# Cross-attention of a streaming encoder layer on one core: weights folded into keys and values per head, token rows run through it once, sample rows moved into the feed-forward layer

## The chip, the cores and the metric

The kernel runs on one core of a Trainium2 chip. The metric is device time in microseconds (us); lower is better. A time is the median of several executions. A profile is of one further execution, and its "span" runs from the first to the last instruction.

The engines: TensorE (PE in the profile, with its weight loads as PEld), VectorE (DVE), ScalarE (ACT), GpSimd (POOL) and SyncE (SP), which here only issues DMAs.

## What is computed

One layer of an encoder, for 2048 prompt rows and 32 sample rows of width 1024: a mixer (band attention with 8 heads beside gated linear attention with 4 heads, and an output projection w_o), cross-attention to 256 memory tokens, and a SwiGLU feed-forward layer of width 2816. Each part is normed before and after and added to the rows. The change is in the cross-attention:

```python
def mem_kv(mem, g_mem, w_mk, w_mv):          # prompt; the sample rows have cached k, v
    m = rmsnorm(mem, g_mem)
    k = (m @ w_mk).reshape(n, 256, 4, 256)   # 4 heads of 256
    v = (m @ w_mv).reshape(n, 256, 4, 256)

def mem_attention(h, k, v, w_mq, w_mo):
    q = (h @ w_mq).reshape(n, t, 4, 256)
    s = einsum('nqhd,nkhd->nhqk', q, k) * 256 ** -0.5
    p = softmax(s)
    o = einsum('nhqk,nkhd->nqhd', p, v).reshape(n, t, 1024)
    return o @ w_mo

xp = xp + rmsnorm(mem_attention(rmsnorm(xp, g_pre_mem), mk, mv, w_mq, w_mo), g_post_mem)
xp = xp + rmsnorm(swiglu(rmsnorm(xp, g_pre_ffn), ...), g_post_ffn)
```

The keys and values of the memory are outputs too. Everything is f32.

## The kernel before

**Arithmetic.** Nearly every product is three matmuls (`mm3`): each f32 operand is split into a rounded part hi (type fp32r) and a rest lo, and hi\*hi + hi\*lo + lo\*hi is summed in PSUM. A split (L424, L425; L429, L430 in place) is a cast on ACT and a subtraction on DVE or POOL. Some small products run on plain f32 operands; the trace shows each of those as two records.

**Order.** Nothing runs in the order of the text. `Order` (top of the file) reads all traced instructions, gives each a cost and a latency, and schedules them onto the engines in passes, by the length of what follows. It respects how many buffers a tag has, the order in which the tiles of one tag are allocated, and memory: a pool that lies where a closed pool lay waits until that pool's work is done. The resulting order is then fixed for each engine, SP's DMA queue included. `high_priority` sets only the first pass's priorities.

**Stages**, with their times in the trace:

1. Input projections (`fm_unit`, `tm_unit`), to about 580 us.
2. The band stage, to about 1275 us: four row blocks (`BLK`, 512, 512, 512, 544 rows), each with band attention (`band_group`: tiles s, pt, po), linear attention (`gla_tile`: g_...), and dense work that a hand-written loop sprinkles between the units in "steps". In block 0 that is the memory's keys and values (`mem_kv`, tiles mkps and mvps); in blocks 1 to 3 it is the output projection of the block before (`out_proj`, wops), which ends in two norms and stores the rows (`x1d`) and the normed rows (`h1d`).
3. Behind the loop: `mem_q0`, the memory queries of the first 416 rows, and `out_proj` of block 3, to 1352 us.
4. The memory stage, 1352 to 1821 us, over five blocks of 416 rows (`CB`; 32 of the last are the sample rows). `mem_q` projects the next block's queries with w_mq (mqps) and stores them to DRAM; `mem_attn` runs, per head, scores of tiles of 104 rows (ms), softmax (mst, mpr), transposes (mpt) and values (mpv); `mem_out` multiplies by w_mo (mops), and `mem_fin` norms twice and stores rows (`x2d`) and normed rows (`h2d`). The weights w_mq and w_mo are loaded and split anew in every block (`load_w`, `w_piece`): 16 pieces of 128x512 per matrix and block. Heads and next queries are woven together in the text.
5. The feed-forward layer, from 1822 us, in three blocks (`CF`) of two column halves (348 or 346), with a seven-product scheme for 2x2 blocks (`seven_mov`, `seven_sta`; tiles pg, pu, pd). Its weights pass through four raw buffers (tag `wraw`, pool cwr) and eight split ones (`wsp`). Seven operands mf, each with a pool of its own, are made from `h2d` before a block starts.

## Time and profile before

| | us |
|---|---|
| median of 3 runs | 3236.2 |
| lowest and highest | 3235.85, 3237.94 |
| the profiled execution | 3241.13 |
| its span | 3239.3 |
| PE busy in the span | 3110.5 |
| the five stages end at about | 580, 1275, 1352, 1821, 3239 |

The profile's views used here: the page (shares of the engines, the chain of work that ended last, groups of instructions), the groups by line in a window, windows (busy time of each engine in a stretch), and the timeline of one engine. A group's row has the line, engine, operation, `out<-in` by the program's names, shape and count; then busy time and the mean length of one in ns; then the engine's idle time just before and who ended it. A timeline row has start and length in us, and in brackets the idle time before it. Matmuls overlap: a matmul's own length is more than its distance from the next one.

### The profile page before, as it was taken

The numbers are of one execution on the slowest core, as the hardware profiler recorded it, in microseconds if no ns is written. First come the engines' busy times: TensorE is split into PE (matmuls) and PEld (weight loads), VectorE is DVE, ScalarE is ACT, GpSimd is POOL, SyncE is SP. The second block draws the span as 40 slices with busy tenths as digits, with TensorE's granted clock in tenths as the row PEclk, the third lists the DMA queues.
The fourth block names the chain that finished last, engine by engine and source line by source line (L and its number), as shares of the span: only waits on it lengthen the run. The fifth ranks groups of instructions, "written<-read, shape, count | busy, mean of one in ns | idle before, by whom it ended". The sixth has DMA issues, their size and how long they took to land.

```text
span 3239.3 us, 57597 instructions
## 1 busy us (share of the span) xinstructions
PE 3110.5 (96%) x21027; PEld 2969.1 (92%) x21027; DVE 2448.5 (76%) x4513; ACT 1709.8 (53%) x3656; POOL 751.6 (23%) x912
## 2 busy tenths in 40 slices
PE   7898999799999999999999799999999999999998
PEld 7888999698888888999999799999889999999997
DVE  7875976476575756678776988888987778987776
ACT  5654655556576756566655554444443334543333
POOL 0200100245374546411010111111041111121111
PEclk9999999999999999999999899999999999999999
DMA  5559374785585756766653644544454445444444
GB/s 149 179 159 298 103 208 130 253 250 181 173 273 165 222 175 200 226 203 207 202 180 118 198 159 167 172 166 166 146 201 143 143 143 170 116 167 144 143 143 161
DMA packets 515261, 575.44 MB, mean 178 GB/s; under 512 B 81952, under 2 KB 431305, under 8 KB 514977
## 3 DMA queue, kind: packets, MB, share of 16 engines
q1 hardware_dynamic: 514977, 571.76, 55.9%
q8 instruction: 166, 2.72, 0.4%
q14 instruction: 118, 0.97, 0.1%
HBM read 422.21 MB, written 150.53 MB: 177 GB/s over the span
## 4 chain that ended last, share of the span: by engine, by line
PE 86%; DVE 5%; DMA 3%; issue 2%; ACT 2%; SPq 1%; POOL 1%; DVEq 0%; POOLq 0%; ACTq 0%
PE pg_X L485 7%; PE pu_X L485 7%; PE pdX L485 7%; PE wops L1330 6%; PE mops L485 6%; PE mqps L485 4%; PE po L1064 4%; PE pg_Y L485 4%; PE pu_Y L485 4%; PE pdY L485 3%; PE s L1059 2%; PE pt L1084 2%; PE pg_Z L485 2%; PE pu_Z L485 2%; PE g_s L1264 2%
## 5 line engine op out<-in xcount | busy, mean ns | idle before, releaser
L425 POOL TENSOR_TENSOR u<-g,u 128x692 fp32r<-128x692 f32 (+1 forms) x111 | 199.0, 1799 | 1043.3 <-ACT u L424 862.6
L485 PE MATMUL pg_X<-mf,wg_s 128*128 128x346 f32 (+1 forms) x1584 | 281.6, 325 | 12.8 <-DVE mf L425 6.3
L485 PE MATMUL pu_X<-mf,wu_s 128*128 128x346 f32 (+1 forms) x1584 | 278.9, 323 | 1.4 <-DVE up L533 1.0
L485 PEld LDWEIGHTS pg_X<-mf,wg_s 128*128 128x128 f32 x1584 | 258.8, 191 | 17.0 <-DVE mf L425 6.6
L485 PEld LDWEIGHTS pu_X<-mf,wu_s 128*128 128x128 f32 x1584 | 257.9, 190 | 2.6 <-DVE up L533 1.3
L485 PE MATMUL pdX<-u,wd 128*128 128x346 f32 (+1 forms) x1440 | 241.2, 326 | 10.3 <-issue 7.3
L485 PEld LDWEIGHTS pdX<-u,wd 128*128 128x128 f32 x1440 | 234.8, 192 | 12.6 <-issue 8.3
L424 ACT CAST wg_s<-wg_r 128x512 fp32r<-128x512 f32 x231 | 136.7, 620 | 191.1 <-DVE wg_r L530 91.7
L1330 PE MATMUL wops<-om,wo_s 128*128 128x512 f32 (+1 forms) x960 | 214.4, 362 | 0.4 <-POOL om L430 0.4
L424 ACT CAST u<-g 128x692 fp32r<-128x692 f32 (+1 forms) x111 | 84.2, 773 | 231.2 <-PE pdX L485 171.7
L485 PE MATMUL mops<-mo,wmo_s 128*128 128x416 f32 x960 | 192.1, 353 | 2.1 <-DVE y L1672 2.1
L425 DVE TENSOR_TENSOR wu_s<-wu_r,wu_s 128x512 fp32r<-128x512 f32 x231 | 166.9, 746 | 27.3 <-ACT wu_s L424 27.1
L424 ACT CAST wu_s<-wu_r 128x512 fp32r<-128x512 f32 x231 | 136.9, 621 | 86.1 <-DVE wu_r L530 38.2
L485 PEld LDWEIGHTS mops<-mo,wmo_s 128*128 128x128 f32 x960 | 177.3, 188 | 5.0 <-issue 3.4
L425 DVE TENSOR_TENSOR wg_s<-wg_r,wg_s 128x512 fp32r<-128x512 f32 x231 | 155.1, 693 | 31.5 <-ACT wg_s L424 31.1
L485 PE MATMUL mqps<-m,wmq_s 128*128 128x416 f32 x768 | 164.4, 359 | 5.3 <-DVE m L430 5.3
L1330 PEld LDWEIGHTS wops<-om,wo_s 128*128 128x128 f32 x960 | 149.3, 188 | 20.4 <-issue 2.2
L1064 PE MATMUL po<-prt,v 128*128 128x128 f32 x1120 | 158.7, 282 | 2.2 <-DMA v<-vad 1.3
L1064 PEld LDWEIGHTS po<-prt,v 128*128 128x128 f32 x1120 | 146.0, 195 | 10.1 <-issue 2.2
L485 PEld LDWEIGHTS mqps<-m,wmq_s 128*128 128x128 f32 x768 | 141.0, 191 | 6.9 <-DVE m L430 5.5
L485 PE MATMUL pg_Y<-mf,wg_s 128*128 128x346 f32 (+1 forms) x792 | 141.1, 326 | 1.7 <-ACT wg_s L424 1.4
L533 DVE TENSOR_TENSOR acc<-acc,pdX 128x346 f32<-128x346 f32 (+1 forms) x192 | 96.4, 513 | 59.1 <-PE pdX L485 58.6
(468 smaller groups left out, 7807.1 us busy)
## 6 DMA issues: line engine op xcount, KB each, us to landing
wd<-wdd SPq DMA_DIRECT2D x140, 512.0 KB, 4.8
wdd<-wd SPq DMA_DIRECT2D x70, 512.0 KB, 3.2
wg_r<-in_w_ffn_gate_dram SPq DMA_DIRECT2D x66, 512.0 KB, 4.4
wu_r<-in_w_ffn_up_dram SPq DMA_DIRECT2D x66, 512.0 KB, 4.7
wmq_r<-in_w_mq_dram SPq DMA_DIRECT2D x80, 256.0 KB, 3.3
wmo_r<-in_w_mo_dram SPq DMA_DIRECT2D x80, 256.0 KB, 3.3
q<-qd SPq DMA_DIRECT2D x32, 512.0 KB, 4.9
wo_r<-in_w_o_dram SPq DMA_DIRECT2D x64, 256.0 KB, 4.0
```

Source lines behind the costliest of these rows:

```text
L424: ACT.copy(hi, src)
L425: (lo_eng or DVE).tensor_tensor(out=lo, in0=src, in1=hi.bitcast(F32), op=ALU.subtract)
L485: PE.matmul(ps, lhsT=a, rhs=b, start=first and i == 0, stop=last and i == len(seq) - 1, skip_group_check=skip)
L533: eng.tensor_tensor(out=out, in0=a, in1=b, op=ALU.add)
L1059: PE.matmul(ps_out, lhsT=q[:, 2 * i + e, q0 : q0 + nq], rhs=ks[:, e, k0 : k0 + ncol], start=i == 0, stop=i == 1)
L1064: PE.matmul(po[:, e * P : e * P + n], lhsT=v[:kk, j, e * 64 : e * 64 + P], rhs=prt[:kk, j, :n], start=j == 0, stop=j == len(rows) - 1)
L1084: PE.transpose(ptp[:kk, j, :n], pr[:n, c0 : c0 + kk], ident[:n, :n])
L1264: PE.matmul(sps[bk, li, :], lhsT=lh, rhs=rh, start=True, stop=True)
L1330: PE.matmul(ps, lhsT=a, rhs=b, start=i == 0, stop=i == len(seq) - 1)
```

## The change

For head h let Wq_h be the 256 columns of w_mq that make its queries, and Wo_h the 256 rows of w_mo that take its output. The scores are h Wq_h k_h^T, so `keys_fold` forms Wq_h k_h^T (1024x256) once for each head; the four together are `gT`, 1024x1024. The output is p_h v_h Wo_h, so `values_fold` forms v_h Wo_h (256x1024) once for each head; the four together are `hT`. Both are split and stay in SBUF (64 KB of each partition apiece). The host passes w_mq a second time, transposed, and the values come out transposed.

- In the band loop only the keys remain in block 0's dense work. The split operand of the memory goes to DRAM (`mmd`) and is read again; the value projection runs behind the loop. `mem_q0` goes. The folding of the keys is woven into the last `out_proj`, the folding of the values follows, then that block's norms.
- The memory stage runs over the 2048 prompt rows alone: `token_tile` takes 128 rows through scores (two halves of 512 columns, two heads each), softmax and transposes; `output` takes 256 rows through the product with hT, the two norms and the stores. `output` comes one quarter late, and its two norm parts are placed between later token tiles.
- The 32 sample rows are handled by `sample()`, a generator advanced once after each `gate_up` of the feed-forward's first block. It multiplies with plain f32 operands and the rows as the stationary side (32 columns), K chunks going in turn to the four partition quarters of one PSUM bank; the quarters are summed by a product with a stacked identity (`fold`). Its weights pass through the feed-forward's raw buffers.
- Pools may now lie at either end of the memory (`side="right"`), so that what follows lies over what is free first. The last two operands' pools (cm5, cm6) lie over the outputs y, four others (cm1 to cm4) mostly over hT. The DRAM blocks `CB` become those of the feed-forward, whose first operands are made in one go of 1392 columns instead of two of 696.
- `Order` learns of the two ends, of several new tiles of one tag in an instruction, and prices a plain f32 matmul of 512 columns and 32 result rows as one of four that run side by side.

The core of the diff:

```diff
+                if n == 512 and list(outs[0].ap)[0][1] == 32:
+                    return n * 0.42, 300.0
...
-    CB = [(i * 416, 416) for i in range(5)]
+    CF = [(0, 348), (696, 346), (1388, 346)]
+    CB = [(s, 2 * n) for s, n in CF]
...
+            return [first] + [partial(key, m) for m in range(KT)], [again] + [partial(value, m) for m in range(KT)]
+        def keys_fold(h):
+            kt = fold_head(mkd, h, "kt")
+            for a in range(2):
+                w = fold_w(ins["w_mq_t"], h, a, "wqt")
+                for i2 in range(2):
+                    ps = psc.tile([P, 512], F32, tag="sc", name=f"gps{h}{a}{i2}")
+                    for i in range(2):
+                        c0 = (2 * i2 + i) * P
+                        mm3(ps[:, i * NMEM : i * NMEM + NMEM], [((w[j][0][:, 0, c0 : c0 + P], w[j][1][:, 0, c0 : c0 + P]), (kt[:, 0, j * NMEM : j * NMEM + NMEM], kt[:, 1, j * NMEM : j * NMEM + NMEM])) for j in range(2)])
...
+        def values_fold(h):
+            vt = fold_head(mvd, h, "vt")
+            for a in range(2):
+                w = fold_w(ins["w_mo"][0], h, a, "wov")
+                for t in range(2):
+                    ps = psc.tile([P, 512], F32, tag="sc", name=f"hps{h}{a}{t}")
+                    mm3(ps, [((vt[:, 0, j * NMEM + t * P : j * NMEM + t * P + P], vt[:, 1, j * NMEM + t * P : j * NMEM + t * P + P]), (w[j][0][:, 0], w[j][1][:, 0])) for j in range(2)])
...
-        for _ in steps(q0 + outp[3][0] + outp[3][1]):
+        for _ in steps(vals):
+            pass
+        att.close()
...
+        for _ in steps(outp[3][0] + weave(outp[3][1], [partial(keys_fold, h) for h in range(HM)])):
+            pass
+        amm.close()
+        kh_ = pool("bhm", 1, **RT)
+        hT = kh_.tile([P, 2, KT, D], F32R, name="hT")
+        for _ in steps([partial(values_fold, h) for h in range(HM)]):
...
+        def token_tile(i, c, pT):
+            ht = load_h(i, c)
+            cs = slice(c * P, c * P + P)
+            row = kvp.tile([P, 2, 512], F32, tag="kv", name=f"mpr{i}_{c}")
+            for hf in range(2):
+                ps = psc.tile([P, 512], F32, tag="sc", name=f"ms{i}_{c}_{hf}")
+                gs = slice(hf * 512, hf * 512 + 512)
+                mm3(ps, [((ht[:, 0, k], ht[:, 1, k]), (gT[:, 0, k, gs], gT[:, 1, k, gs])) for k in range(KT)])
+                st = sp.tile([P, 8], F32, tag="st8", name=f"mst{i}_{c}_{hf}", bufs=4)
+                pr = row[:, hf]
+                softmax(pr, ps, P, st, 2)
+                tr = ptr.tile([P, 4, P], F32, tag="tr", name=f"mpt{i}_{c}_{hf}")
+                for j in range(4):
+                    PE.transpose(tr[:, j], pr[:, j * P : j * P + P], ident)
+                if c == 0:
+                    pT.append(tp.tile([P, 2, HK, 256], F32R, tag="pT", name=f"pT{i}_{hf}"))
+                split(pT[hf][:, 0, :, cs], pT[hf][:, 1, :, cs], tr, DVE)
...
+            for m4 in range(2):
+                pss = [py.tile([P, 512], F32, tag="out", name=f"mo{i}_{2 * m4 + j}") for j in range(2)]
+                for e in range(2):
+                    for hf in range(2):
                         for j in range(2):
+                            c = slice((4 * m4 + 2 * j + e) * P, (4 * m4 + 2 * j + e) * P + P)
+                            mm3(pss[j][:, e * 256 : e * 256 + 256], [((hT[:, 0, hf * HK + k, c], hT[:, 1, hf * HK + k, c]), (pT[hf][:, 0, k], pT[hf][:, 1, k])) for k in range(HK)], hf == 0, hf == 1)
...
+        for i in range(NQ):
+            pT = []
+            token_tile(i, 0, pT)
+            for f in fins:
+                next(f, None)
+            token_tile(i, 1, pT)
+            for f in fins:
+                next(f, None)
+            if pend is not None:
+                fins = [output(i - 1, pend)]
+                next(fins[-1], None)
+            pend = pT
...
+        mps = {i: pool(f"cm{i}", 1, **RT) for i in range(5)}
...
+        mps.update({i: pool(f"cm{i}", 1) for i in (5, 6)})
...
+            def proj(src, mov, name):
+                part = uu.tile([P, 2, 512], F32, tag="u", name=name + "_p")
+                for hf in range(2):
+                    ps = pd.tile([P, 512], F32, tag="dense", name=f"{name}_a{hf}")
+                    for k2 in range(KT // 2):
+                        w = wr.tile([P, 2, 512], F32, tag="wraw", name=f"{name}w{hf}{k2}", bufs=WRB)
+                        SP.dma_start(w, src[2 * k2 * P : (2 * k2 + 2) * P, hf * 512 : hf * 512 + 512].rearrange("(k p) m -> p k m", p=P))
+                        for e in range(2):
+                            j = (2 * k2 + e) % 4
+                            PE.matmul(ps[j * TS : j * TS + TS], lhsT=mov[:, 2 * k2 + e], rhs=w[:, e], start=k2 < 2, stop=k2 >= 2)
+                    (DVE.tensor_copy if hf else ACT.copy)(part[:, hf], ps)
+                ps = pd.tile([P, 512], F32, tag="dense", name=name)[:, : KT * TS].rearrange("p (m t) -> p m t", m=KT)
+                for m in range(KT):
+                    PE.matmul(ps[:, m], lhsT=part[:, m // HK, m % HK * P : m % HK * P + P], rhs=fold, start=True, stop=True)
+                return ps
...
             for g in range(NG):
                 held.append(gate_up(g))
+                next(own, None)
```

More of the change, by code (lines that the diff above doesn't have):

```diff
@@ L296, in _pass @@
                         _, i = heappop(heap)
-                        stop = None
-                        for k in self.uses[i]:
+                        stop, new = None, {}
+                        for k in sorted((k for k in self.uses[i] if not held[k]), key=place.get):
                             g = self.tag[k]
-                            if not held[k] and (free[g] <= 0 or head[g] != place[k] or (back is None and self.first[k] != i)):
+                            c = new.get(g, 0)
+                            new[g] = c + 1
+                            if free[g] <= c or head[g] + c != place[k] or (back is None and self.first[k] != i):
                                 stop = g
@@ new lines, in value @@
+            def value(m):
+                w = load_w(wp, ins["w_mv"][0], m * P, P, f"wmv{m}")
+                ps = pd.tile([P, 512], F32, tag="dense", name=f"mvps{m}")
+                yield from mm3_steps(ps[:, :NMEM], [(w[k], (mv[k][:, 0, :NMEM], mv[k][:, 1, :NMEM])) for k in range(KT)], 12)
+                vf = sp.tile([P, 544], F32, tag="st", name=f"mvf{m}")
+                DVE.tensor_copy(vf[:, :NMEM], ps[:, :NMEM])
+                SP.dma_start(mvd[m * P : (m + 1) * P, :], vf[:, :NMEM])
+                SP.dma_start(outs["mv_t"][m * P : (m + 1) * P, :], vf[:, :NMEM])
@@ new lines, in softmax @@
+        def softmax(pr, ps, n, st, heads):
+            DVE.tensor_reduce(out=st[:n, 0:heads], in_=ps.rearrange("p (h j) -> p h j", h=heads), axis=AX.X, op=ALU.max, negate=True)
+            for h in range(heads):
+                c = slice(h * NMEM, h * NMEM + NMEM)
+                ACT.activation(pr[:n, c], ps[:, c], AF.Exp, bias=st[:n, h : h + 1], accum_out=st[:n, 2 + h : 3 + h])
+            DVE.reciprocal(st[:n, 4 : 4 + heads], st[:n, 2 : 2 + heads])
+            for h in range(heads):
+                c = slice(h * NMEM, h * NMEM + NMEM)
+                DVE.tensor_scalar(out=pr[:n, c], in0=pr[:n, c], scalar1=st[:n, 4 + h : 5 + h], scalar2=None, op0=ALU.mult)
@@ new lines, in encoder_step @@
+        NQ = TP // 256
+        pend, fins = None, []
+        for i in range(NQ):
[10 more added lines that the diff above has]
+            pend = pT
+        fins.append(output(NQ - 1, pend))
+        for f in fins:
+            for _ in f:
+                pass
@@ L1809, in encoder_step @@
+        own = sample()
         late = []
```

453 lines of the change are left out of this document (218 added, 235 removed).

## The prediction

> **What bounds the kernel now.** First the shares of the engines and the chain that ended last (the page's parts 1 and 4):
>
> ```profile
> PE 3110.5 (96%) x21027; PEld 2969.1 (92%) x21027; DVE 2448.5 (76%) x4513; ACT 1709.8 (53%) x3656; POOL 751.6 (23%) x912
> PE 86%; DVE 5%; DMA 3%; issue 2%; ACT 2%; SPq 1%; POOL 1%; DVEq 0%; POOLq 0%; ACTq 0%
> ```
>
> TensorE is busy for 96% of the span and makes up 86% of the chain. But "busy" here includes matmuls that overlap their own tails, so I check it stage by stage. The windows below cover the first band block, the passage to the last w_o projection, the memory stage, the passage to the feed-forward layer, and its first block:
>
> ```profile
> 590.00:758.00 168.00, 156.42 (x1542) 138.19 (x1543) 118.03 (x322) 106.76 (x306) 76.67 (x168) 0.97 0.76 239
> 1255.00:1352.00 97.00, 96.79 (x674) 94.37 (x673) 53.29 (x88) 54.63 (x120) 38.29 (x33) 1.00 0.75 236
> 1352.00:1821.00 469.00, 461.37 (x2660) 444.73 (x2658) 360.27 (x682) 281.09 (x643) 74.23 (x57) 0.99 0.62 188
> 1821.00:1846.00 25.00, 9.49 (x26) 7.22 (x27) 24.46 (x33) 14.08 (x23) 3.82 (x2) 0.55 0.46 127
> 1846.00:2300.00 454.00, 446.75 (x2747) 440.86 (x2746) 400.11 (x657) 211.75 (x389) 73.94 (x41) 0.99 0.49 168
> ```
>
> The columns are the length, then the busy time and count of PE, PEld, DVE, ACT and POOL, then the granted clock, the DMA share and GB/s. The change replaces the 469 us of the memory stage. These are its matmul groups, from the groups by line in that window:
>
> ```profile
> L485 PE MATMUL mops<-mo,wmo_s 128*128 128x416 f32 x960 | 192.1, 353 | 2.1 <-DVE y L1672 2.1
> L485 PE MATMUL mqps<-m,wmq_s 128*128 128x416 f32 x768 | 164.4, 359 | 5.3 <-DVE m L430 5.3
> L485 PE MATMUL ms<-kTp,q 128*104 128x256 f32 (+1 forms) x456 | 73.6, 289 | 0.1
> L485 PE MATMUL mpv<-prR,vTp 128*128 128x416 f32 (+1 forms) x240 | 56.1, 352 | 0.0
> ```
>
> What one matmul costs is its distance from the next, not its own 350 ns. I read that from unbroken runs in the timeline of PE (start, length, operation, count):
>
> ```profile
> 1274.68 29.77 PE L1330 MATMUL mqps<-hq,wmq_s 128*128 128x416 f32 x156
> 1304.28 48.10 PE L1330 MATMUL wops<-om,wo_s 128*128 128x272 f32 x384
> 1352.22 0.92 PE L485 MATMUL mqps<-m,wmq_s 128*128 128x416 f32 x4
> ...
> 1364.58 1.57 PE L485 MATMUL ms<-kTp,q 128*104 128x256 f32 x12
> 1365.99 2.80 PE L485 MATMUL mqps<-m,wmq_s 128*128 128x416 f32 x14
> ...
> 1721.28 1.05 PE L1636 MATMUL ms<-ksT,qf 128*32 128x256 f32 x4
> 1722.26 0.44 PE L1645 MATMUL mpt<-ident,mpr 128*128 128x128 f32 x2
> ...
> 1734.00 0.53 PE L1655 MATMUL mpv<-prT,vs 128*128 128x32 f32 x4
> ```
>
> - 416 columns: (1304.28 - 1274.68) / 156 = **0.1897 us**. 272 columns: (1352.22 - 1304.28) / 384 = 0.1248. So a column costs 0.00045 us, and 512 columns extrapolate to **0.233**, 384 to 0.175.
> - 256 columns: (1365.99 - 1364.58) / 12 = **0.1175**.
> - Matmuls on plain f32 operands show as two records each. Two of 256 columns took 1722.26 - 1721.28 = 0.98, so **0.49** each. Two of 32 columns took 0.53 with their tail; I take 0.2 each.
>
> The old stage adds up: 768 x 0.1897 = 145.7 (queries of blocks 1 to 4), 960 x 0.1897 = 182.1 (w_mo), 456 x 0.1175 = 53.6 (scores), 192 x 0.1897 + 48 x 0.175 = 44.8 (values), 7.1 for the sample rows (8 x 0.49 + 16 x 0.2), and some 25 for transposes and all-ones matmuls. That is 458 of 469 us, so the stage is filled with matmuls almost throughout, and removing matmul time there removes span.
>
> **The change, part by part.** PE work that goes: queries 960 x 0.1897 = 182.1 (block 0's 192 run before 1352), w_mo 182.1, scores 53.6, values 44.8, sample rows 7.1: **469.7 us**.
>
> PE work that comes:
> - prompt scores against the folded keys, 16 tiles x 2 halves x 8 x 3 = 768 of 512 columns: 179.0;
> - outputs against the folded values, 8 quarters x 8 x 8 x 3 = 1536 of 256 columns: 180.5;
> - the folds, 192 of 256 columns (22.6) and 96 of 512 (22.4).
>
> Together **404.5 us**, 65 less. The 160 transposes and ten all-ones matmuls become 128 and sixteen shorter ones; I take these as equal. The value projection (192 of 256 columns, 22.6) keeps its size and moves behind the band.
>
> The sample rows come back in the feed-forward layer: 64 plain f32 matmuls of 32 result rows and 512 columns, 32 of 32 columns (6.4), 8 of 256 (3.9), transposes and norms 1.5. The 64 are the large unknown. One after another they cost 2 x 0.49 = 0.98 each, **63 us**. They write to the four partition quarters in turn; side by side in fours they cost **16**. The trace has small matmuls on separate parts of the array, and narrow ones on 32 rows of result:
>
> ```profile
> 551.86 1.56 PE L485 MATMUL wvb_T<-wvb_s,tail 128*32 128x256 f32 x12
> 553.25 1.57 PE L485 MATMUL wvb_T<-wvb_sx,tail 128*32 128x256 f32 x12
> 554.66 4.42 PE L485 MATMUL wvb_Y<-wvb_s,mi 128*128 128x256 f32 x36
> ...
> 1233.39 0.85 PE L1264 MATMUL g_s<-g_W 64*64 64x64 f32 x22
> ```
>
> The g_s records on 64x64 quarters start (0.85 - 0.22) / 21 = 0.03 us apart, the 0.22 being one record's own length. Serially, a plain f32 record of 64 columns would take 0.98 / 4 / 4 = 0.061. So they do run beside each other, at least two at a time, which puts the 64 near 31 us. Records as short as 0.03 us may be held by issue rather than by the array, so I go below that row, to **20**. The Trainium skill, "TensorE: Matmul & The Clock Gate", Part 3, gives three column tiles of 32 at N=512 a speedup of 2.38. An estimate by it, with four tiles at the same efficiency (3.2), would also be 20; no run here shows that form.
>
> Sample rows in all 31.8, so PE has 65 - 32 = **33 us** less.
>
> DVE and ACT lose the repeated splits of w_mq and w_mo, which each block made anew:
>
> ```profile
> L425 DVE TENSOR_TENSOR wmo_s<-wmo_r,wmo_s 128x512 fp32r<-128x512 f32 x80 | 55.8, 703 | 22.1 <-ACT wmo_s L424 20.6
> L425 DVE TENSOR_TENSOR wmq_s<-wmq_r,wmq_s 128x512 fp32r<-128x512 f32 x62 | 48.0, 780 | 14.6 <-ACT wmq_s L424 13.7
> ```
>
> Of DVE's 360 us in the stage these are 104; the folds need 32 such splits, some 23 us. Softmax and norm work per token stays, so DVE has about 280 us beside 405 of PE, and PE stays the bound. In the feed-forward's first block DVE is at 400 of 454 us; the sample rows bring some 40 short instructions, about 10 us (estimate: 0.25 each, from the 0.35 and 0.42 of 256 columns quoted under the rivals), in a stage that they lengthen by more. That costs nothing; with that cover gone it costs those 10. SP loses 160 weight loads of 256 KB for 32 such and 16 of 512 KB, and gains eight of 512 KB by which the projection's operand goes out and comes back; its queue holds 1% of the chain. The 16 pass through the four raw buffers of the gate and up weights, so a late sample matmul holds a gate load behind it; the planner sees this, and I put nothing on it.
>
> **Stalls that go, and that come.** These waits stand in the stage now:
>
> ```profile
> 1374.24 7.77 PE L485 MATMUL mqps<-m,wmq_s 128*128 128x416 f32 x26 [5.27 <-DVE m L430]
> ...
> 1797.23 14.40 PE L485 MATMUL mops<-mo,wmo_s 128*128 128x416 f32 x75 [2.07 <-DVE y L1672]
> ...
> 1833.62 1.82 PE L485 MATMUL pg_X<-mf,wg_s 128*128 128x348 f32 x5 [6.25 <-DVE mf L425]
> ...
> 1842.26 1.76 PE L448 MATMUL n_ps<-n_acc,ones 128*128 128x416 f32 x2 [5.66 <-POOL n_acc L446]
> ```
>
> After the 5.27 us wait, 26 matmuls took 7.77 us where 4.9 is their price, so that wait costs 8.2 us in all. The wait at 1797 costs 2.1. In the window from 1821 to 1846 PE issued 26 records, worth about 5 us at the next window's 454 / 2747 = 0.165: **20 us** lost. Sum 30.
>
> What comes:
> - First band block: the value projection was 22.6 us of filling in a window where PE is the busiest engine with 156 of 168 us. If PE holds that block, moving it costs 0; if the linear-attention chain does, up to 22.6. PE being ahead of DVE's 118, I take **6**.
> - Before the last w_o projection PE had 29.6 us of queries to do (the row at 1274.68) while its operands came:
>
> ```profile
> 1292.11 10.78 POOL L430 TENSOR_TENSOR om<-om 128x544 fp32r<-128x544 f32 x7 [0.26 <-ACT om L429]
> ```
>
>   The first of them is ready at 1292, so from 1274.7 some 18 us need filling. There are 22.6 us of values (part used earlier) and one key fold (5.7); the later folds queue behind w_o's weights. 0 to 18, I take **3**.
> - Start of the token tiles: a tile's operand (load, ACT, POOL) comes just as the tile before it ends; 0 to 8, I take **3**.
> - Passage to the feed-forward: its operands lie where the folded values lay, and the last two where the outputs lie that the last quarter's two norms still need. Their eight casts and subtractions of 1392 columns start only with the last output matmul. I keep the 20 of now; the sample query projection, whose buffers are free earlier, can run in that gap, and I let it fill 8. **12** (0 to 30).
>
> Sum 24 against 30. The span changes by -33 - 6 = -39. The profiled execution took 3241.1 us and lies 4.9 above the median of 3236.2 us, so 3241.1 - 39 - 4.9 = **3197 us**.
>
> **Rivals.** (a) The column tiles run one after another: 63 instead of 20, so 3240. For it: the 128x32 rows at 551.86 cost as much per matmul as 128x128 ones; against it: those all lie on one quarter, and g_s overlaps. (b) Each change of tile shape empties the array. One record outlasts its pitch by about 0.16 us (350 ns against 190); if the planner alternates the 64 with full matmuls, 128 changes cost 20, so 3217. Against it: 12 narrow ones at 551.86 and 12 at 553.25 take 1.39 and 1.41, just 12 x 0.1175, so no drain shows at these borders. The Trainium skill, "TensorEngine Tiling (Array Packing)", Key Properties, states that drain as a rule; here the trace doesn't agree. (c) The gain goes back into holes: the band block keeps its time (+17) and the 18 us stay empty (+15): 3229. (d) **Slower**: the softmax chain paces the token loop. Per half tile it is a reduction, two exponentials, a reciprocal and two scalings:
>
> ```profile
> L1638 DVE TENSOR_REDUCE mst<-ms 128x1 f32<-128x256 f32 x12 | 5.0, 422 | 5.2 <-PE ms L485 5.1
> L1640 ACT ACTIVATE mpr<-ms,mst 128x256 f32<-128x256 f32 x12 | 5.7, 475 | 1.1 <-DVE mst L1638 0.8
> L1642 DVE TENSOR_SCALAR mpr<-mpr,mst 128x256 f32<-128x256 f32 x12 | 4.2, 353 | 0.4
> ```
>
> With two of each, transposes and the split of 512 columns this is about 4.7 us, and there are 32 halves. Above 39 / 32 = 1.2 us exposed per half the gain is gone; at half the chain, 2.4 us, it costs 75: 3272. Against it: the same chain is hidden now (0.1 us of idle before 456 score matmuls, 0.0 before mpv), and three score banks and a whole quarter of output work lie beside it. (e) More than forecast: no holes, and the passage filled: 3197 - 24 = 3173.
>
> **How the numbers follow.** Forecast 3197 with its own range 3180 to 3215: 0.50. (a) 0.10, (b) 0.06, (c) 0.14, (d) 0.09, (e) 0.11. A difference of 0.2% (6.5 us) is about what a measurement of this kernel can tell. Faster: forecast, (b), (e) and most of (c), 0.77. Same: (a) and the rest of (c), 0.14. Slower: (d), 0.09. The range of 3168 to 3238 leaves out (d), half of (a) and a little below (e), 0.18.
>
> **What would show it.** Between the band and the first pg_X the new profile should hold 768 score matmuls near 0.233 apart and 1536 output matmuls near 0.1175, with few idle entries; the 64 narrow matmuls should start about 0.25 to 0.3 us apart; the window of the passage should hold a gap near 12 us; wops of block 0 should start 15 us or more before 758. The forecast is wrong if the narrow matmuls stand near 1 us apart, if idle time on DVE or ACT stands before the transposes of the token tiles, or if that first w_o projection starts no earlier than now.

## The result, and the profile after

| | before | after |
|---|---|---|
| median of 4 runs, us | 3236.45 | 3201.76 |
| lowest and highest | 3235.85, 3237.94 | 3201.33, 3202.80 |
| span of the profiled execution | 3239.3 | 3199.6 |

The ratio is 0.9893, with a 95% interval of 0.9875 to 0.991: 34.7 us less, where 39 were forecast (3197). The profiled execution of the kernel before lay 4.7 us above its median, so the spans differ by more, 39.7. The sum came out near; the account below shows that several of its terms did not.

From the page of the kernel after (engines: busy time, share of the span, instructions; then the chain's shares by engine; then two groups):

```profile
PE 3076.3 (96%) x21091; PEld 2884.7 (90%) x21091; DVE 2303.6 (72%) x4226; ACT 1584.9 (50%) x3338; POOL 770.5 (24%) x912
...
PE 88%; DVE 6%; ACT 2%; DMA 2%; issue 1%; SPq 1%; POOL 0%; DVEq 0%; ACTq 0%; POOLq 0%
...
L471 PE MATMUL ms<-gT,hm 128*128 128x512 f32 x768 | 190.5, 401 | 1.7 <-POOL hm L436 1.5
L471 PE MATMUL mo<-pT,hT 128*128 128x256 f32 x1536 | 191.4, 283 | 0.1
```

PE is still the engine that the chain runs on. The two last rows are the new memory stage: 768 score and 1536 output matmuls, as counted, with 1.8 us of idle time before all of them. PE's longest waits in the token tiles name a norm's sum (acc, 3.0 us in all) and a tile's operand (hm, 1.5); the softmax is named once, with 0.2 us, so rival (d) did not come. Four stretches of the same kernel, as windows (columns as in the prediction: length, PE, PEld, DVE, ACT, POOL, clock, DMA share, GB/s):

```profile
1357.80:1747.10 389.30, 384.60 (x2464) 345.60 (x2465) 194.08 (x373) 133.02 (x297) 89.86 (x55) 1.00 0.35 106
...
1747.10:1776.60 29.50, 23.91 (x128) 21.41 (x126) 28.51 (x42) 18.68 (x30) 7.28 (x4) 0.94 0.34 112
1747.10:2259.20 512.10, 493.03 (x2947) 463.81 (x2946) 426.33 (x696) 233.01 (x423) 72.40 (x41) 0.98 0.50 167
2259.20:2728.30 469.10, 453.02 (x2790) 449.21 (x2790) 374.11 (x603) 197.38 (x356) 83.53 (x53) 0.98 0.47 153
```

They are the token tiles, the passage to the feed-forward layer, its block 0 (the passage is its beginning), and its block 1. Cut at marks that both kernels have (the first wops, ms and pg_X matmul, read from the timelines), the 39.7 us between the two spans fall like this. "Forecast" puts the prediction's own terms into these stretches:

| stretch of the span | before, us | after, us | change | forecast |
|---|---|---|---|---|
| start to the first w_o matmul | 758.0 | 722.2 | -35.8 | -16.6 (values -22.6, band +6) |
| to the first score matmul | 595.0 | 635.6 | +40.6 | +34.2 (values +22.6, folds +45, block 0's queries -36.4, hole +3) |
| token tiles | 469.6 | 389.3 | -80.3 | -81 (matmuls -433.3 and +359.5, stalls -10.3 and +3) |
| feed-forward block 0 | 480.1 | 512.1 | +32.0 | +24 (sample rows +31.8, passage -8) |
| the rest | 936.6 | 940.4 | +3.8 | 0 |

The token tiles are right to within 1 us. The first two stretches are off by 19 and 6 in opposite directions, block 0 by 8. Of the -35.8, 2.7 us lie in the input projections, which end at 583.0 and 580.3: their matmuls are the same, and in the fourteen profiles here that mark lies anywhere from 578.8 to 584.3. The experiments take up the rest.

### The profile page after: what moved, and what is told of

Its sections match the earlier page's. It is cut to its first block, busy times and chain, and to the rows that moved or that the text cites. A ratio compares the mean times of both kernels' runs of the same rounds, so it can differ in the third digit from the quotient of the medians.

```text
span 3199.6 us, 56225 instructions
## 1 busy us (share of the span) xinstructions
PE 3076.3 (96%) x21091; PEld 2884.7 (90%) x21091; DVE 2303.6 (72%) x4226; ACT 1584.9 (50%) x3338; POOL 770.5 (24%) x912
## 4 chain that ended last, share of the span: by engine, by line
PE 88%; DVE 6%; ACT 2%; DMA 2%; issue 1%; SPq 1%; POOL 0%; DVEq 0%; ACTq 0%; POOLq 0%
PE pu_X L471 8%; PE pg_X L471 7%; PE pdX L471 7%; PE wops L1327 6%; PE ms L471 5%; PE mo L471 5%; PE po L1061 4%; PE pu_Y L471 4%; PE pg_Y L471 4%; PE pdY L471 4%; PE s L1056 2%; PE pt L1081 2%; PE pu_Z L471 2%; PE pg_Z L471 2%; PE g_s L1261 2%; PE pdZ L471 2%
## 5 line engine op out<-in xcount | busy, mean ns | idle before, releaser
L471 PE MATMUL ms<-gT,hm 128*128 128x512 f32 x768 | 190.5, 401 | 1.7 <-POOL hm L436 1.5
L471 PE MATMUL mo<-pT,hT 128*128 128x256 f32 x1536 | 191.4, 283 | 0.1
L471 PEld LDWEIGHTS mo<-pT,hT 128*128 128x128 f32 x1536 | 185.7, 188 | 1.6 <-DVE my L1661 0.3
L471 PEld LDWEIGHTS ms<-gT,hm 128*128 128x128 f32 x768 | 142.5, 189 | 34.8 <-POOL hm L436 1.9
L471 PE MATMUL pu_Y<-mf,wu_s 128*128 128x346 f32 (+1 forms) x792 | 138.3, 322 | 0.3 <-ACT pu_c L560 0.3
```

Of the source, the lines that this page charges most:

```text
L471: PE.matmul(ps, lhsT=a, rhs=b, start=first and i == 0, stop=last and i == len(seq) - 1, skip_group_check=skip)
```

## The experiments

**First question: why did the band's first block lose 36 us, not 17?** Theory: the whole value projection was filling in that block; moving it takes its 22.6 us out, and something else takes the rest. Three kernels try that. In the first, the kernel before gets only the move.

`before_values_late`

```diff
-dense = [(steps(kv1 + kv2), 2 + 8 * 2 + 4 * 4), ...
+dense = [(steps(kv1), 1 + 8 * 2), ...
-for _ in steps(q0 + outp[3][0] + outp[3][1]):
+for _ in steps(kv2 + q0 + outp[3][0] + outp[3][1]):
```

> The kernel before with one thing of the change alone: its 192 value matmuls (22.6 us) run behind the band loop instead of in the first band block. In the changed kernel the first w_o projection starts 36 us earlier, 13 more than these matmuls are worth. Theory 1, the values stood in front of the block's attention work in PE's queue and held it up beyond their own time: the first w_o projection starts near 722 us, the projection behind the loop costs 22.6, and the time is about 3223. Theory 2, they are only moved: first w_o projection near 735, time 3236 within 3. Theory 3, the extra 13 come from other parts of the change (pools at two ends, the planner's new rules): first w_o projection later than 735 or near 758 and a time above 3236.

Measured: 3253.82 us, ratio 1.0054 (1.0039 to 1.0069), 17 us slower than before. The first w_o matmul came at 740.8, 17 us earlier and not 36; counted from the end of the input projections the block took 162.2 us in place of 175.0, 12.8 less. At its new place the projection stretched over 47.6 us, for matmuls worth 22.6. PE's waits there (engine, line, whom it waited for, us in total, times, longest):

```profile
PE mvps L1330 <- ACT mm L424: 4.8, 4, 3.3
PE mvps L1330 <- DVE mvf L1426: 3.9, 6, 1.2
```

Its operands are made a second time there, and one PSUM bank passes from product to product through a DVE copy. The band's gain was given back behind it. So the move alone explains neither the 36 us nor the gain, as theory 3 had it.

`after_values_early`: the kernel after, with the projection back in the first block.

```diff
-dense = [(steps(kv), 1 + 8 * 2), ...
+dense = [(steps(kv + vals), 2 + 8 * 2 + 8 * 2), ...
-for _ in steps(vals):
-    pass
```

> The changed kernel with the value projection back in the first band block. Theory 1 (it holds up the block): first w_o projection back near 758 us, and behind the loop 22.6 us less; with the hole before the last w_o projection that the values fill now (between 0 and 18 us) the time is 3215 to 3230. Theory 2 (only moved): 3202, or up to 3215 if that hole opens.

Measured: 3216.78 us, ratio 0.994 (0.9925 to 0.9955), 15 us slower than after. The first w_o matmul moved from 722.2 to 746.2: 24 us, about the projection's own length, so in this kernel PE does hold the block and nothing had to be paid for moving it (the 6 us of the prediction). But 746.2 is still 12 us ahead of the 758.0 of before, with the same matmuls in the block; 10 of the 12 remain when both are counted from the end of the input projections (165.0 us against 175.0). And at the band's end, from the last w_o matmul of block 2 to the first of block 3 (this kernel, then after):

```profile
1210.90:1274.70 63.80, 50.44 (x400) 42.04 (x399) 44.78 (x98) 37.78 (x104) 41.48 (x53) 0.87 0.55 165
```

```profile
1180.20:1254.50 74.30, 70.19 (x607) 62.22 (x606) 58.56 (x125) 47.91 (x126) 39.88 (x52) 1.00 0.72 218
```

Without the values there, PE is busy for 50 of 64 us, with them for 70 of 74. The 22.6 us of values lengthen this stretch by 10.5: they fill the hole that block 0's memory queries filled before. From the first w_o matmul to the first memory score it is 7.0 us (635.6 against 628.6), so of the 24 some 17 are kept in the profiles, 15 in the medians. That much of the gain comes from moving the values.

`before_values_kept`: are the other 10 us the operands that the kernel before scales and splits twice? They are kept here.

```diff
-... [partial(first, 1)] + [partial(value, g) for g in range(4)]
+... [partial(value, g) for g in range(4)]
```

> The kernel before, one edit: the value projection in the first band block reads the memory operands that the key projection has already split, and they are not scaled and split a second time (8 scalings, 8 copies and 8 subtractions go; no matmul goes). Open is why the kernel after begins the first output projection 12 us earlier than before even with its value projection in the same place (746.2 against 758.0). Theory R, the second making of the operands held the first block: the first output projection begins at 746 +- 3 here, and of the 12 us at least a third reaches the end, so 3224 to 3232. Rival P, it is where the pools lie or how the order came out otherwise: the first output projection begins at 758 +- 3 and the time is 3236 +- 3.

Measured: 3236.1 us, ratio 0.9991 (0.9981 to 1.0). The first w_o matmul came at 754.9, but the input projections ended at 579.7 against 583.0, so the block is as long as before (175.2). Theory R falls. Part of the 10 us shows in the first 60 us behind the input projections, in before, in this kernel, in after_values_early and in after:

```profile
583.00:643.00 60.00, 43.75 (x362) 36.11 (x360) 29.39 (x101) 38.01 (x114) 19.36 (x44) 0.91 0.83 271
```

```profile
579.70:639.70 60.00, 44.30 (x356) 37.47 (x354) 28.73 (x97) 37.62 (x115) 19.85 (x45) 0.86 0.80 261
```

```profile
581.20:641.20 60.00, 49.76 (x480) 40.45 (x479) 36.90 (x115) 38.72 (x116) 29.00 (x69) 0.89 0.86 276
```

```profile
580.30:640.30 60.00, 51.26 (x496) 42.08 (x494) 37.94 (x123) 40.72 (x125) 30.67 (x70) 0.91 0.91 290
```

PE is busy for 44 us in the kernels built on before, whatever is done to the values, and for 50 to 51 in those built on after. All of them begin with a hole. In before it lies behind the first score matmuls (timeline of PE):

```profile
582.98 0.56 PE L1059 MATMUL s<-ks,q 128*128 128x128 f32 x4
592.55 1.23 PE L1059 MATMUL s<-ks,q 128*128 128x256 f32 x4 [9.02 <-DVE u_mn L1043]
```

and DVE's wait before it names a transfer:

```profile
DVE u_sb L1043 <- DMA vbd<-wvb_tail: 9.5, 1, 9.5
```

In after it lies ahead of them, with linear-attention matmuls (g_z, g_e) in it, and DVE waits 7.0 us for the load of nb:

```profile
582.76 0.67 PE L1214 MATMUL g_z<-wal,g_ga 17*128 17x256 f32 x2 [2.31 <-DMA g_ga<-glow]
586.20 2.07 PE L1234 MATMUL g_e<-tall,g_laR 128*128 128x512 f32 x4 [2.78 <-ACT g_laR L430]
591.84 0.66 PE L1056 MATMUL s<-ks,q 128*128 128x128 f32 x2 [2.01 <-DMA ks<-kad]
```

So the hole itself is not the difference: in the first 15 us behind the input projections PE is busy for 6.0 in before and for 7.6 in after. The 25 us behind that make most of it, 19.3 against 24.5.

In all, some 10 us are a gain of the change outside the memory attention. The new rule for buffers in the planner's `_pass` is not it: with the old rule put back, the kernel after gets the same order of instructions on every engine, and so does the kernel before with the new one. What is left is where the pools lie (two ends of the memory in place of one stack), and so which pools wait for which; the value projection's new form; and the priorities, which the planner takes from all that follows. None was tried alone, so the cause stays open.

**Second question: what do the sample rows cost in the feed-forward layer, and why?**

`after_no_sample`

```diff
 def sample():
     hs = ...; SP.dma_start(hs, h1d[-1][:, 512:]...)
     yield
+    for dst in (x2d, h2d):
+        SP.dma_start(dst[-1][...], hs)
-    (projections, scores, softmax, outputs, norms of the 32 rows)
```

> The changed kernel without the cross-attention of the 32 sample rows (their rows go to the feed-forward as they are; this leaves out part of the computation). Their matmuls take 27 us of PE in the trace, and gate weights arrive late after them for some 12 us. If both are on the path: 3163. If the sample matmuls stand mostly in gaps that are there anyway (the passage from the memory stage): 3180 to 3195.

Measured: 3159.66 us, ratio 0.9762 (0.9748 to 0.9777), 42 us below after. Block 0 takes 472.9 us from the last output matmul, against 512.1: 39.2. From start to next start, the sample rows' own matmuls take 29.9 of those in the kernel after (15.6 the narrow ones of the projections, 8.2 the 32-column ones, 3.6 the scores, 2.5 transposes, norms and a wait of 0.8). The other 9 us are feed-forward matmuls that stand further apart.

`after_sample_second_block`

```diff
+if b == 1 and g >= 2:
     next(own, None)
```

> The changed kernel with the sample rows' steps in the second block of the feed-forward (at its gate and up steps 2 to 6) instead of the first. In the first block DVE makes the sums of the down weights and is busy for 9 tenths; in the second for 7 to 8. Theory 1, the waits for gate weights after the sample's projections come from a DVE that can't catch up: they shrink, 3188 to 3194. Theory 2, they come from the four raw buffers through which the sample's weights pass in order: they stay, 3200 to 3204. Theory 3, the sample rows fill the passage to the feed-forward now, and that gap opens: above 3204.

Measured: 3193.37 us, ratio 0.9863 (0.9847 to 0.988), 8.4 us below after. The feed-forward blocks 0 and 1 of after_no_sample and of this kernel:

```profile
1750.40:2223.30 472.90, 456.49 (x2790) 446.45 (x2789) 415.80 (x666) 217.32 (x395) 73.02 (x41) 0.99 0.46 158
2223.30:2692.30 469.00, 452.18 (x2790) 448.11 (x2789) 373.95 (x603) 197.71 (x356) 83.70 (x53) 0.97 0.47 153
```

```profile
1749.60:2221.70 472.10, 456.88 (x2790) 446.54 (x2789) 416.92 (x666) 217.35 (x395) 73.53 (x41) 0.99 0.46 158
2221.70:2722.60 500.90, 484.63 (x2947) 458.76 (x2946) 381.64 (x633) 213.64 (x384) 80.88 (x53) 0.99 0.50 165
```

In block 1 the sample rows add 31.9 us, and their own matmuls, with the waits between them, take 31.5: the others take no longer in sum. In block 0 the same work adds 39.2, 9 more than its own matmuls. Theory 1 named the time, and what differs most between the blocks is indeed DVE, busy for 416 of 473 us in one and 374 of 469 in the other; that this is the cause is argued from that alone.

`after_other_ring`: in block 0, where do those 9 us come from? The sample rows' weights go through the ring of split weights here.

```diff
-w = wr.tile([P, 2, 512], F32, tag="wraw", ..., bufs=WRB)
+w = ws.tile([P, 2, 512], F32R, tag="wsp", ..., bufs=WSB).bitcast(F32)
```

> The kernel after, one edit: the sample rows' projection weights land in the ring of eight split weights and not in the ring of four raw ones; the same matmuls, the same loads. Theory W, the 12 to 15 us by which the sample rows cost more than their 27 us of matmul time are gate weights that stand behind sample weights in the four raw buffers: feed-forward block 0 shortens from 512 to 498 to 503 and the time is 3188 to 3194. Rival V, any ring that both share costs the same, or what waits is VectorE and ScalarE for other reasons: block 0 stays at 512 +- 3 and the time at 3202 +- 3. Below that, rival U: the split weights' ring is the tighter one, since its eight are wanted by every gate unit, block 0 over 516, time over 3206.

Measured: 3192.35 us, ratio 0.9859 (0.9844 to 0.9874), 9.4 us below after. Block 0 took 505.4 us: 7 less, where theory W asked for 9 to 14. Of the 7, 3.3 are the sample's own matmuls with the waits between them (26.7 us for 29.9), 3.4 the others, which stand less far apart. So the raw ring is a part of it, and not all. How it works in the kernel after (windows: the sample's query projection, its output projection, and the 60 us behind that):

```profile
1776.60:1796.00 19.40, 18.42 (x96) 10.57 (x96) 7.88 (x11) 3.79 (x6) 0.00 (x0) 1.00 0.87 288
1911.00:1929.00 18.00, 17.20 (x88) 9.08 (x87) 6.00 (x10) 2.65 (x4) 3.33 (x2) 1.00 0.69 214
1929.00:1989.00 60.00, 56.94 (x340) 54.76 (x340) 53.86 (x94) 28.47 (x50) 8.49 (x5) 0.97 0.51 181
```

While sample weights hold the four raw buffers, DVE (fourth column) has 6 to 8 us of work in 18 to 19, since no gate weight is there to split; then it is busy for 54 of 60, which is little more than the 51 of after_no_sample in the same 60 us. Nor does PE idle much longer: 19.1 us of the block, against 16.4 without the sample rows (length less busy time in the rows above) and 18.0 in after_other_ring. The 9 us lie in the distances of matmuls. Some 4 us are matmuls that stand 0.28 to 0.30 us apart in place of 0.16: 55 of them in the block, against 22 in after_no_sample and 22 in after_other_ring. Some 3.6 us are the full matmuls beside a run of the sample's, which stand about 0.25 apart (more on them under the next kernel). The first kind runs at a lower granted clock (third column from the right), behind both projections; in after_other_ring there is none behind either:

```profile
1797.40:1804.10 6.70, 5.59 (x20) 4.91 (x19) 3.31 (x5) 1.59 (x3) 0.00 (x0) 0.50 0.09 29
1930.40:1933.40 3.00, 3.00 (x10) 2.77 (x10) 2.96 (x3) 0.04 (x1) 1.47 (x1) 0.51 0.26 89
```

Gate weights come late there: waits of 0.7 to 1.1 us that name wg_s stand at 1795.82, 1800.29 and 1930.38. So what the ring costs shows as slow matmuls around short waits. Whether DVE's arrears make those waits was not separated from the ring itself.

`after_one_quarter`: do the narrow matmuls run side by side on the four column quarters? All of them write to the first quarter here.

```diff
-PE.matmul(ps[j * TS : j * TS + TS], ..., start=k2 < 2, stop=k2 >= 2)
+PE.matmul(ps[:TS], ..., start=k2 + e == 0, stop=k2 + e == KT // 2)
```

> The changed kernel with all narrow matmuls of the sample rows on the first quarter of the array, so that none can run side by side (the partial sums add up in place; the result is the same). Theory, quarters run side by side: the 64 records take 0.43 each plus the runs' 0.12, about 30 us instead of 15.6, so about 3216, less where a gap takes some of it. Rival, a narrow matmul costs the same wherever it lies and its price is that of its two records: 3202.

Measured: 3217.31 us, ratio 0.9937 (0.9922 to 0.9952), 15.5 us above after. The same runs of narrow records in the kernel after, in this kernel, and (a run of eight) in after_other_ring, each with the row that follows it:

```profile
1776.65 1.91 PE L1835 MATMUL sq_a<-sqw,s_hq 128*32 128x512 f32 x12
1778.49 2.02 PE L471 MATMUL pg_Z<-mf,wg_s 128*128 128x348 f32 x11
1780.44 1.05 PE L1835 MATMUL sq_a<-sqw,s_hq 128*32 128x512 f32 x2
1781.41 1.38 PE L471 MATMUL pu_Z<-mf,wu_s 128*128 128x348 f32 x7
1782.72 1.04 PE L1835 MATMUL sq_a<-sqw,s_hq 128*32 128x512 f32 x2
...
1784.05 1.05 PE L1835 MATMUL sq_a<-sqw,s_hq 128*32 128x512 f32 x4
1785.03 0.43 PE L471 MATMUL pg_X<-mf,wg_s 128*128 128x348 f32 x1
...
1834.71 2.08 PE L471 MATMUL pg_X<-mf,wg_s 128*128 128x348 f32 x12
1836.62 2.08 PE L471 MATMUL pg_Y<-mf,wg_s 128*128 128x348 f32 x12
```

```profile
1779.77 5.34 PE L1835 MATMUL sq_a<-sqw,s_hq 128*32 128x512 f32 x12
1785.04 2.02 PE L471 MATMUL pg_Z<-mf,wg_s 128*128 128x348 f32 x11
...
1790.61 1.90 PE L1835 MATMUL sq_a<-sqw,s_hq 128*32 128x512 f32 x4
1792.44 0.43 PE L471 MATMUL pg_X<-mf,wg_s 128*128 128x348 f32 x1
```

```profile
1794.36 1.07 PE L1835 MATMUL sq_a<-sqw,s_hq 128*32 128x512 f32 x8
1795.35 0.63 PE L1839 MATMUL sq<-s_fold,sq_p 128*128 128x32 f32 x4
```

A matmul is two records. On one quarter, 12 records take 5.27 us and 4 take 1.83: 0.43 each and 0.11 per run ((5.27 - 1.83) / 8, and what is left). On different quarters, 2 records take 0.97, 4 take 0.98, 8 take 0.99: up to four matmuls cost what one does. Twelve (six matmuls, so two on some quarter) take 1.84, which is 4 x 0.43 and the same 0.12. The full matmuls between the runs pay too: twelve among themselves take 1836.62 - 1834.71 = 1.91 us, 0.16 each, but the eleven at 1778.49 take 1.95 and the seven at 1781.41 take 1.31, each 0.19 more than their number at 0.16.

`after_quads`: twelve of the fifteen runs in the kernel after are pairs of matmuls, which leave half the array empty. Pieces of four K chunks by 256 columns make runs of four.

```diff
-for k2 in range(KT // 2): w = wr.tile([P, 2, 512], ...)      # 2 chunks x 512 columns
+for c in range(2):
+    for k4 in range(2): w = wr.tile([P, 4, 256], ...)         # 4 chunks x 256 columns
-if n == 512 and list(outs[0].ap)[0][1] == 32:
+if n in (256, 512) and list(outs[0].ap)[0][1] == 32:
```

> The changed kernel with each raw weight piece of the sample rows holding four K chunks of 256 columns instead of two of 512, so that four quarters of the array get work in one run of matmuls, not two. In the trace a run of two matmuls (4 records) takes 0.98 us, one of six 1.84, one of one 0.97. Theory 1, quarters run side by side in full and a run costs its longest quarter (0.43 per record) plus 0.12: now 16 runs of 0.55, 8.8 us instead of 15.6, so 3195 if nothing else moves. Theory 2, a change of tile shape costs a fixed 0.55 and records then 0.108 each: 16 runs of about 0.98, 15.7, so 3202.

Measured: 3202.14 us, ratio 0.9891 (0.9876 to 0.9906), no different from after. Its narrow matmuls did fall into the same law, 0.57 for 8 records of 256 columns (four matmuls) and 1.00 for 16:

```profile
1786.17 1.07 PE L1836 MATMUL sq_a<-sqw,s_hq 128*32 128x256 f32 x16
1787.17 0.42 PE L471 MATMUL pg_Z<-mf,wg_s 128*128 128x348 f32 x1
1787.52 0.64 PE L1836 MATMUL sq_a<-sqw,s_hq 128*32 128x256 f32 x8
1788.09 1.86 PE L471 MATMUL pg_Z<-mf,wg_s 128*128 128x348 f32 x10
```

They took 9.5 us in place of 15.6, and block 0 505.0 in place of 512.1. But the edited price in the planner changed the order of the whole program: the band's second block took 171.6 us where the kernel after has 165.3, and that ate the gain.

**Third question: does PE's matmul time set the token stage?** In `after_two_products` a third of the output matmuls goes (512 of 256 columns, 60 us at 0.1175).

```diff
-mm3(pss[j][...], [((hT[:, 0, ...], hT[:, 1, ...]), (pT[hf][:, 0, k], pT[hf][:, 1, k])) ...])
+for v in range(2):
+    PE.matmul(pss[j][...], lhsT=hT[:, 0, ...], rhs=pT[hf][:, v, k], ...)
```

> The changed kernel with two of the three products in the outputs of the memory stage (the low part of the folded values is left out, so the result is less exact): 512 matmuls of 0.1175 fewer, 60 us of PE. Theory, PE paces the token loop: 3142, no idle time of PE above 10 us in the stage. Rival, the softmax chain or the norms stand close behind PE: the gain stops early, 3165 to 3190, with idle PE before transposes or outputs.

Measured: 3149.97 us, ratio 0.9728 (0.9714 to 0.9743), 52 us below after. The last output matmul came at 1689.5 after the first score at 1360.5: 329 us, 60 less than the 389. The missing 8 went at the passage: block 0 took 520.6 us from the last output matmul, where after has 512.1. Its first gate unit began 16 us before that matmul, and it waited: to the second unit 76.1 us passed, with PE busy for 63.2, where after has 48.7. Its longest waits there name the norms of the last outputs (n_s on DVE, 6.4 us) and an operand (mf, 3.4). So PE paces the token tiles even without those 60 us, and what follows them is paced by the operands of the feed-forward layer.

**Fourth question: is there a better version?** Three kernels move the sample rows to the second block and add one edit each.

`after_second_quads` (both edits of after_quads, price included):

> Both edits of the sample rows together: second block of the feed-forward, and four K chunks to a piece. If the waits for gate weights and the half empty array are separate costs, the two gains add: 3180 to 3188. If they are the same cost (fewer, longer runs), no more than the better of the two alone.

Measured: 3200.97 us, ratio 0.9888 (0.986 to 0.9917), runs from 3195.95 to 3211.48. The longer second band block came back with the edited price (171.5 us), and feed-forward block 1 took 503.4.

`after_second_quads_old_price`:

> The kernel after with the sample rows moved to the second feed-forward block and their narrow matmuls in fours, one to each column quarter, with the planner's price as it was (the band's order is then unchanged, where the earlier kernel with both edits had a new one). Theory: the two gains add when the band stays: block 1 from 500.9 to 492 to 496 and the time from 3193.4 to 3185 to 3190. Rival: in the second block the raw buffers of four chunks come one after the other anyway and nothing more is gained: block 1 at 500 +- 3, time 3193 +- 3.

Measured: 3188.27 us, ratio 0.9847 (0.9832 to 0.9861), the lowest of all full kernels, though its interval overlaps that of after_sample_second_block. The number met the theory and the mechanism did not: block 1 took 501.3 us, not 492 to 496. PE's waits in it:

```profile
PE so_a L1836 <- DMA sow<-in_w_mo_dram: 4.5, 4, 2.4
PE pg_Z L471 <- ACT wg_s L430: 3.9, 1, 3.9
PE pdX L471 <- POOL u L431: 3.6, 1, 3.6
PE sq_a L1836 <- DMA sqw<-in_w_mq_dram: 1.3, 2, 1.2
```

The matmuls in fours now wait for the loads of their weights (4.5 and 1.3 us); the rival was right there. The 5 us by which the medians differ do not come from the edit as far as the profiles show: the two profiled executions differ by 7.8 us, all of it ahead of block 1 (6.0 up to the last output matmul), where both kernels have the same order of matmuls. What makes that difference stays open.

`after_second_halves`:

```diff
     (DVE.tensor_copy if hf else ACT.copy)(part[:, hf], ps)
+    yield
```

> The kernel after with the sample rows moved to the second feed-forward block and each of their two projections spread over two gate steps (half of the output columns in each). If what is left beyond the matmul time there (32 us in block 1 for 27 us of matmul time) is gate weights behind sample weights, block 1 falls from 500.9 to 496 to 498 and the time to 3188 to 3191. If it is the narrow matmuls running in ones and twos, nothing changes: block 1 at 501 +- 2, time 3193 +- 2, or a little more by new breaks.

Measured: 3206.32 us, ratio 0.9905 (0.9889 to 0.9922). Block 1 took 502.4 us, so spreading the loads gained nothing; and the last block's first three gate units took 122.6 us where after_sample_second_block has 111.5. Neither side expected that. The sample rows' last norm ends at 2671 there in place of 2509, still 49 us ahead of the last block; the cause of the longer block stays open.

## Why the prediction came out, step by step

- **"PE work that goes" and "comes", 469.7 and 404.5: right.** The stage changed by -80.3 against -81. The prices were the extrapolated 0.233 and the 0.1175. From the timeline of PE in the kernel after, with the row behind each run (between rows left out):

```profile
1595.36 8.41 PE L471 MATMUL ms<-gT,hm 128*128 128x512 f32 x35
1603.61 1.59 PE L471 MATMUL mo<-pT,hT 128*128 128x256 f32 x12
...
1609.13 17.38 PE L471 MATMUL mo<-pT,hT 128*128 128x256 f32 x146
1626.35 5.77 PE L471 MATMUL ms<-gT,hm 128*128 128x512 f32 x24
```

  (1603.61 - 1595.36) / 35 = 0.236, and (1626.35 - 1609.13) / 146 = 0.118. Two-product outputs confirm it from the other side.
- **"First band block ... I take 6": wrong, the value in the new kernel is 0.** PE held that block; moving the values took out 24 us. In the kernel before the same move took out 12.8, so there more than 6 would have had to be paid. A further 10 us went that no step had, most of it at the band's start, which the prediction didn't look at; 2 to 3 us are a profile of before whose input projections ended late.
- **"Before the last w_o projection ... I take 3": too low.** The stretch to the token tiles grew by 40.6 against 34.2. The values stand there as forecast and fill most of the hole; what is left is 4 idle us beside them and matmuls further apart.
- **"64 plain f32 matmuls": miscounted.** They are 16 per projection, 32 in all, and 64 records. Two errors met, by luck: the 32 took 15.6 us, 0.49 each, where 20 was forecast for 64, 0.31 each. One after another, 32 would by the prediction's 0.98 be 31 us, so rival (a)'s 3240 was never open; on one quarter they took 29.3 and the whole kernel 3217. That they overlap was right. Four in one run take 0.99, where by the prices on one quarter they would take 8 x 0.43 + 0.11 = 3.55: a factor of 3.6, near the 3.2 that the prediction estimated from the Trainium skill, "TensorE: Matmul & The Clock Gate", Part 3. But the planner made pairs, at half of that. In all the sample rows took 29.9 us, against 31.8.
- **Rival (b), a drain at each change of tile shape: its price came, its count didn't.** A run of narrow matmuls costs 0.12 us beyond its records, and the full matmuls beside it cost 0.19 more: 0.31 for two changes, so about 0.16 each, as rival (b) had it. But the 32 narrow matmuls stand in fifteen runs, so there are 30 changes and not 128: under 5 us, not 20. The rule in the Trainium skill, "TensorEngine Tiling (Array Packing)", Key Properties, that a change of tiling mode drains the array, agrees with these rows, unlike those at 551.86. Part of it is not the shape: behind the sample's plain f32 matmuls of full shape the next full one also stands 0.24 to 0.28 away, though ahead of them it stands 0.16 away and ahead of the narrow ones 0.25.
- **"A late sample matmul holds a gate load behind it ... I put nothing on it": the step that failed.** In block 0 the sample rows cost 9 us more than their own matmuls. Sending their weights through another ring made the block 6.7 us shorter, 3.4 of it in the other matmuls; another 3.6 of the 9 are the changes of rival (b). The cover that the prediction named for DVE ("in a stage that they lengthen by more") is not there while the sample weights hold the raw buffers: DVE then has 6 to 8 us of work in 18 to 19.
- **"Passage ... 12": nearly right in size, wrong in reason.** In the passage window PE issued 122 feed-forward matmuls, worth 20.1 us at the prediction's 0.165, and four of two norms (1.8, with a wait of 0.8); of 29.5 us some 8 were lost, where before lost 20. The sample's query projection does not fill it: it begins at 1776.65, behind the gap.
- **The rest, 0: 3.8.** Blocks 1 and 2 are longer by 3.5 and 0.3 although nothing in them changed but the place and the sharing of buffers; this stays open.

Of what would show it: the two matmul distances and the first w_o matmul (36 us earlier) came as announced. The narrow matmuls, announced 0.25 to 0.3 us apart, were 15.6 / 64 = 0.24 apart by record and 0.49 by matmul, which hid the miscount. Rival (c) came in one place, the hole that the values only partly fill; (e) did not.

The net: -19 from the band's first block, +6 in the stretch behind it, +8 in block 0 and +4 in the rest, against the forecast; they cancel to within 1 us of the span. That they cancel is luck, and a few us of the first are the profile of before, which ran 4.7 us above its median: by the medians the change is 34.7 us where 39 was forecast.

## What to carry to other kernels

A stage that PE fills can be priced by counting matmuls and reading the distance between starts from an unbroken run; that part was right to 1 us in 389. What has to be priced beside it is each buffer ring that the new work shares with work already there, and each change between kinds of matmul: 16 loads through the four raw buffers came with 9 us beyond the new matmuls themselves, less through another ring, and none in sum in a block where VectorE has more room. And where one planner orders the whole program, look for the gain in every stretch before believing a term: here 10 of 35 us came from a stretch that the change doesn't name.

## What the runs showed of the hardware

- Plain f32 matmuls with 32 result rows, written to different quarters of the output partitions, run fully side by side: one to four of 512 columns take 0.97 to 0.99 us together, and those on one quarter add up (0.86 us each). A single narrow matmul is as dear as four.
- The same narrow matmuls between full ones cost about 0.12 us more per run than their records, whatever the length of the run, and the full ones beside the run another 0.19.
- In three stretches of feed-forward block 0 behind the sample rows' matmuls the granted clock was 0.50 to 0.53, and full matmuls stood 0.29 us apart in place of 0.16.
